# The second query projection of a decoder layer as a seven-product unit, placed behind the first scores

## The chip, the cores and the metric

One core of a Trainium2 chip runs the whole kernel. The metric is the device time of one execution in microseconds; the kernel before takes 1145.6 us (median of 3 runs, 1145.52 to 1145.76). Line numbers are those of the kernel before.

## The reference

One decoder layer on 512 tokens of width 1024 in float32: half a SwiGLU step, a token mixer, half a second SwiGLU step, and a gated per-layer embedding. The change is in the mixer:

```
h = rmsnorm(x, mix_norm);  z = h @ w_in
zq, zk, zv, zc, zg = split(z)            # 1024, 128, 128, 2048, 2048 columns
q = rope(rmsnorm(zq per head)); k = rope(rmsnorm(zk per head))
a = sliding_window_attention(q, k, zv, sinks) @ attn_proj     # 16 heads of 64, window 128
u = ca * sigmoid(cb); c = silu(layernorm(depthwise_conv(u, 31 taps))) @ conv_proj
x = x + (sigmoid(ga) * a + sigmoid(gb) * c) @ w_out
```

The 16 query heads are computed as two groups of 8 heads (g = 0 and 1), each a product of 512 tokens x 1024 features with 1024 x 512 weights.

## The kernel before

**Arithmetic.** A float32 product is made of three passes (`mm3`, line 758): every operand is split into a rounded high part and a remainder (`split_into`, line 718: one ScalarE copy, one VectorE subtraction), and high x high, high x low and low x high are added up in PSUM. Weights come in pieces of 128 x 1024 (512 KB): `piece` (line 733) loads one and splits it; for the keys named in `FLEX` (line 55), the queries among them, the subtraction goes to VectorE or GpSimd, whichever is free.

**Two ways to make a product.** `token_major` (line 1326) makes one directly: for each of 8 blocks k of 128 features and each of 4 token tiles, the activations are the weights of TensorE and 512 columns of the piece stream past. `unit` (line 987) makes a product of 2 x 2 blocks with seven block products in place of eight (in the manner of Strassen and Winograd). It loads four pieces, adds two of them together by accumulating DMAs on GpSimd's queue, makes two further sums on VectorE into PSUM tiles `zs`, and splits the seven weight forms. Its activations come as seven `forms`, which are sums of quarters of the input. Two accumulators a and b for each of two m, four PSUM banks, are filled step by step, and after each step the caller reads what is done (`yield`). With `turned=True` the token tile is TensorE's weight and 256 columns of the weight form stream past.

**The queries.** `queries(g)` (line 1418) uses `query_unit` (line 1377) for g = 0 and `token_major` with four pieces of `wq` for g = 1 (PSUM tile `q1b`, read by four ScalarE copies into `zq`). `query_unit` builds the forms of the mixer's input itself: the sums `mix_t4` to `mix_t7` of quarters of the scaled input, split into `mix_f`, and the parts of `h2` (the trace calls them `mix_h`). It then runs the unit named `wq0` (PSUM tiles `wq_a`, `wq_b`, `zs_wq`) and scales its results by the norm's factor into `zq`. In both ways `heads_rsqrt` (line 1301: four squares on ScalarE, four sums on VectorE and some fifteen tiny steps) and `rope` (line 1316: GpSimd) follow. `scores` (line 1436) transposes a token tile of `zq` and multiplies it with the keys; it takes one bank and then four. `softmax` (line 1483) and `values` (line 1503) follow. The convolution (`conv`, line 1279) of five blocks of 128 channels is a chain of 31 VectorE steps each in a PSUM bank (`cz`, at most two at once), and that of three (`POOLCH`) is made of ScalarE products and GpSimd sums. `conv_norm` (line 1578) adds the blocks (`ln_acc`), takes the mean (`ln_mb`) and the variance (`ln_v`), and makes the operand `cv` of the projection `cp`.

**Order.** The code first records all operations of the program as a list. `ORDER` (line 40) says in which order the mixer's steps are recorded: K keys and values, a and b the two conv projections of a block, Q queries, A scores, E softmax, V values, g and h the two gates, p attention projection, L the layer norm. A planner (`plan`, line 676) then simulates the list with a cost for each operation and due times taken back from the matmuls (`deadlines`, line 378); TensorE's next group is the first of the next 10 (`WINDOW`) whose operands and banks are there, and the other engines take the most urgent ready operation. Buffers are numbered slots (`SLOTS`, line 686): 70 activation tiles of 128 x 512, four raw pieces, four high and four low weight pieces, two raw pieces of kind k, 8 PSUM banks. The planner repeats this in a few passes, keeps the best, and the real program is issued in the order of its start times. So a changed step changes the place of any other.

**Layout.** `_layout` (line 1783) stores the weights in the host's memory in the order in which pieces are read. For the first query group (`wq[:4]`) these are the four blocks of the 2 x 2 product; for the second they are rows of 512 columns.

Of the kernel before, what the change touches and what calls it, by code (L numbers as in the profile page):

```python
# [16 lines left out]
P = 128  # L17
S = 512
NT = S // P
D = 1024  # L20
# [3 lines left out]
NH = 16  # L24
NKV = 2
HD = 64
# [7 lines left out]
PIECE = 1024  # L34
# [3 lines left out]


ORDER = """  # L40
K0 a0 b0 a1 b1 Q0 A0 a3 a2 A1 b2 E0 E1 b3 A2 E2 a4 V0 A3 a5 E3 V1 b4 Q1 V2 b5
V3 A5 a7 A6 g5 h7 A4 E5 A7 E6 E4 V6 g3 a6 E7 g0 V5 b6 V4 g4 g6 V7 h1 g2 h4 b7
g1 p0 p2 g7 p3 L0 p4 h3 p7 h2 p5 p1 p6 h5 h0 h6
"""
# [365 lines left out]
CUT = 4  # L410
PLAIN = 6, 4
MID = 20, 20
DOWNS = {8: [(0, 4)], 20: [(4, 11)]}
SPARE = 0, 1, 2, 4

# [273 lines left out]
def record():  # L689
# [74 lines left out]
    def part(w, s):  # L764
        return w[0][:, s], w[1][:, s]
# [608 lines left out]

    zq, rq = {}, {}

    def query_unit(g):

        forms = {f: [] for f in range(1, 8)}
        for q in range(2):  # L1380
            t5, t6, t7, t4 = (ftile(f"mix_t{n}_{q}") for n in (5, 6, 7, 4))
            for j in range(2):
                k, v = 2 * q + j, slice(j * HS, (j + 1) * HS)
                xg = ftile(f"mix_xg{k}")
                nc.scalar.activation(xg, x[k], AF.Copy, scale=g_mix[:, k : k + 1])
                gb, xb = g_mix[:, k + 4 : k + 5], x[k + 4]
                nc.flex.tensor_tensor(t5[:, v], xg[:, lo_], xg[:, hi_], op=ALU.subtract)
                nc.vector.scalar_tensor_tensor(t6[:, v], xb[:, hi_], gb, t5[:, v], op0=ALU.mult, op1=ALU.add)
                nc.vector.scalar_tensor_tensor(t7[:, v], xb[:, hi_], gb, xg[:, hi_], op0=ALU.mult, op1=ALU.subtract)
                nc.vector.scalar_tensor_tensor(t4[:, v], xb[:, lo_], gb, t6[:, v], op0=ALU.mult, op1=ALU.subtract)  # L1390
                for f, i, t in ((1, k, lo_), (2, k + 4, lo_), (3, k + 4, hi_)):
                    forms[f].append(part(h2[i], t))
            for f, t, sign in ((5, t5, None), (6, t6, -1.0), (7, t7, None), (4, t4, -1.0)):
                parts = split(f"mix_f{f}_{q}", t, sign)
                for j in range(2):
                    forms[f].append(part(parts, slice(j * HS, (j + 1) * HS)))

        def src(b):
            return Dram("wq")[4 * g + 2 * (b // 10 - 1) + b % 10 - 1]

        for t in range(NT):
            zq[g, t] = ftile(f"zq{g}_{t}")
        for f, m, b1, b2 in unit(f"wq{g}", src, PIECE, lambda k, m: k * HS, forms, turned=True):
            z0, z1 = zq[g, m], zq[g, m + 2]
            r0, r1 = (r2k[:, t : t + 1] for t in (m, m + 2))
            if f == 1:
                nc.scalar.activation(z0[:, lo_], b1, AF.Copy, scale=r0)
                nc.vector.scalar_tensor_tensor(z0[:, lo_], b2, r0, z0[:, lo_], op0=ALU.mult, op1=ALU.add)
            elif f == 6:
                nc.scalar.activation(z1[:, lo_], b2, AF.Copy, scale=r1)  # L1410
                nc.scalar.activation(z1[:, hi_], b1, AF.Copy, scale=minus[:, m + 2 : m + 3])
            elif f == 7:
                nc.vector.scalar_tensor_tensor(z1[:, lo_], b1, r1, z1[:, lo_], op0=ALU.mult, op1=ALU.add)
                nc.vector.scalar_tensor_tensor(z1[:, hi_], b2, minus[:, m + 2 : m + 3], z1[:, hi_], op0=ALU.mult, op1=ALU.add)
            else:
                nc.scalar.activation(z0[:, hi_], b2, AF.Copy, scale=minus[:, m : m + 1])

    def queries(g):

        if g == 0:  # L1420
            query_unit(g)
        else:
            pss = token_major(f"q{g}", "wq", 4 * g, 4, 2, S)
            for t in range(NT):
                z = zq[g, t] = ftile(f"zq{g}_{t}")
                nc.scalar.activation(z, pss[t], AF.Copy, scale=r2k[:, t : t + 1])
        z3s = [zq[g, t].rearrange("p (h d) -> p h d", d=HD) for t in range(NT)]
        rq[g] = heads_rsqrt(f"q{g}", z3s, 8, HD**-0.5, False)
        for t in range(NT):
            rope(f"q{g}_{t}", z3s[t], 8, qcs, t)  # L1430
# [237 lines left out]
    forms = {f: [] for f in range(1, 8)}  # L1668
# [25 lines left out]
    for oo in range(1):  # L1694
# [6 lines left out]
        for f, m, b1, b2 in steps:  # L1701
            o = 2 * oo + m
# [80 lines left out]
def _layout(inputs):  # L1783

    import numpy as np

    f = {k: np.asarray(v) for k, v in inputs.items()}

    def feat(v):
        return v.reshape(KD, P).T  # L1790

    def kxn(w):

        kt, nt = w.shape[0] // P, w.shape[1] // P
        return w.reshape(kt, P, nt, P).transpose(2, 1, 0, 3).reshape(nt, P, kt * P)

    def wgu(w):
        v = w.reshape(2, 4, P, 2, KF, P)
        return v.transpose(4, 0, 2, 1, 3, 5).reshape(2 * KF, P, PIECE)

    def wdown(w):


        v = w.reshape(KF // 2, 2, P, 2, 2, 2, P)
        out = np.zeros((24, P, 8, P), np.float32)
        out[:8] = v[:4].transpose(4, 3, 1, 2, 5, 0, 6).reshape(8, P, 8, P)
        out[8:, :, :7] = v[4:].transpose(4, 5, 3, 1, 2, 0, 6).reshape(16, P, 7, P)
        return out.reshape(24, P, PIECE)

    order = [h for j in range(NPAIR) for h in (j, j + NPAIR)]  # L1810
    win = f["w_in"][0]
    o = np.cumsum([0, NH * HD, NKV * HD, NKV * HD, 2 * D, 2 * D])
    wq = win[:, : o[1]].reshape(D, NH, HD)[:, order].reshape(4, 2, P, 2, S)
    wq = wq.transpose(3, 0, 2, 1, 4).reshape(8, P, PIECE)
    w0 = win[:, : o[1]].reshape(D, NH, HD)[:, order][:, :8].reshape(2, 4, P, 2, S // 2)
    wq[:4] = w0.transpose(3, 0, 2, 1, 4).reshape(4, P, PIECE)
    wkv = win[:, o[1] : o[3]].reshape(2, 4, P, 2 * P).transpose(0, 2, 1, 3).reshape(2, P, PIECE)

    def pairs(w):
        t = kxn(w)  # L1820
        n = t.shape[0] // 2
        return t.reshape(2, n, *t.shape[1:]).transpose(1, 0, 2, 3).reshape(t.shape)

    wap = f["attn_proj"][0].reshape(NH, HD, D)[order].reshape(NH * HD, D)

    half = HD // 8
    inv = np.float32(500000.0) ** (-np.arange(0, 16, 2, dtype=np.float32) / np.float32(16))
    ang = np.arange(S, dtype=np.float32)[:, None] * inv[None, :].astype(np.float32)
    cos, sin = np.cos(ang), np.sin(ang)
    cs = np.stack([np.concatenate([cos, cos], 1), np.concatenate([-sin, sin], 1)], 1)  # L1830
    cs = cs.astype(np.float32).reshape(NT, P, 2, 2 * half).transpose(1, 0, 2, 3)

    qi, kj = np.arange(W)[:, None], np.arange(W)[None, :]
    masks = np.where(kj > qi, -1e30, 0.0).astype(np.float32)

    rows = lambda v: np.broadcast_to(v, (P, v.shape[-1]))
    gains = np.stack(
        [
            feat(f[k][0])
            for k in (  # L1840
                "ffn1_norm", "mix_norm", "ffn2_norm", "ple_gate_norm",
                "ple_norm", "dw_b", "conv_ln_g", "conv_ln_b",
            )
        ],
        1,
    )
    arrays = {
        "xT": f["x"][0].T.reshape(KD, P, S),
        "pT": f["p"][0, 0].T.reshape(KP, P, S),
        "gains": gains,  # L1850
        "wgu1": wgu(f["ffn1_wgu"][0]),
        "wd1": wdown(f["ffn1_wdown"][0]),
        "wgu2": wgu(f["ffn2_wgu"][0]),
        "wd2": wdown(f["ffn2_wdown"][0]),
        "wq": wq,
        "wkv": wkv,
        "wzc": pairs(win[:, o[3] : o[4]]),
        "wzg": pairs(win[:, o[4] : o[5]]),
        "gq": rows(f["q_norm"][0]),
        "gk": rows(f["k_norm"][0]),  # L1860
        "sinks": rows(f["sinks"][0][order]),
        "wap": kxn(wap),
        "dww": f["dw_w"][0].T.reshape(KD, P, TAPS).transpose(1, 0, 2),
        "wcp": kxn(f["conv_proj"][0]),
        "wout": f["w_out"][0].reshape(2, 4, P, 2, 2, 2, P).transpose(4, 3, 0, 2, 5, 1, 6).reshape(8, P, PIECE),
        "wple": kxn(f["ple_proj"][0]).reshape(2, 4, P, KP * P).transpose(0, 2, 1, 3).reshape(2, P, PIECE),
        "wgate": np.concatenate(
            [
                f["ple_gate_w"][0].reshape(2, 4, P, 2, 2, 2, P).transpose(4, 3, 0, 2, 5, 1, 6).reshape(8, P, PIECE)[:4],
                kxn(f["ple_gate_w"][0])[[2, 3, 6, 7]],  # L1870
            ]
        ),
        "cs": cs,
        "masks": masks,
    }
    return {k: np.ascontiguousarray(v) for k, v in arrays.items()}
# [19 lines left out]
```

## Time and profile before

| | us |
|---|---|
| median of 3 runs | 1145.6 |
| the profiled execution | 1145.5 |
| its span | 1143.8 |
| TensorE (PE) busy | 1135.7 |
| VectorE (DVE) busy | 1000.4 |
| ScalarE (ACT) busy | 743.0 |
| GpSimd (POOL) busy | 457.8 |

The span is the time from the first to the last instruction in the trace; some 1.7 us lie around it. All instructions bear one line (1778), where the planned list is issued, so groups are told apart by tiles. In the trace the first feed-forward step ends near 345 us, the mixer near 705, its output product follows, and the second feed-forward step ends near 1083. A matmul's printed duration includes its pipeline, so successive matmuls overlap and the spacing of starts is what counts.

### The profile page before, as it was taken

To read this page: it belongs to the slowest core of one execution; us is meant where nothing else is said; L and a number is where in the kernel's file an instruction comes from. 1 tells how busy PE (TensorE), PEld (TensorE's weight loads), DVE (VectorE), ACT (ScalarE), POOL (GpSimd) and SP (SyncE) were. 2 spreads that over 40 slices of the span, in tenths; PEclk is the share of its full clock that TensorE was granted. 3 is DMA by queue.
4 is the path that set the end of the run, shared out by engine and by line. 5 is a ranking of instruction groups with operands and counts; after the bars stand their busy time and mean duration, and the time that the engine had idled before them with its cause. 6 is when DMAs were issued, how large, how long until landed. Compare 5 with 4: busy or idle time off the path is not lost.

```text
span 1143.8 us, 20799 instructions
## 1 busy us (share of the span) xinstructions
PE 1135.7 (99%) x7804; PEld 1054.2 (92%) x7804; DVE 1000.4 (87%) x1701; ACT 743.0 (65%) x1332; POOL 457.8 (40%) x531
## 2 busy tenths in 40 slices
PE   9999999999999999999999999999999999999998
PEld 8899999999999988888888888988999999999997
DVE  7799978889887799997997779989998788899897
ACT  7656456665557889999975654655663566565682
POOL 1632113322112896976688124035231132131156
PEclk9999999999999999999999999999999999999999
DMA  7456666665658481664644554436666666656643
GB/s 242 126 162 148 165 160 163 151 144 151 157 132 208 119 206 38 173 158 97 162 129 131 146 148 108 114 108 169 145 164 151 150 167 148 168 119 178 152 117 99
DMA packets 54821, 167.92 MB, mean 147 GB/s; under 512 B 6592, under 2 KB 14400, under 8 KB 54720
## 3 DMA queue, kind: packets, MB, share of 16 engines
q1 hardware_dynamic: 39888, 114.12, 30.2%
q0 software_dynamic: 14688, 52.44, 26.6%
q8 instruction: 61, 1.00, 0.4%
q14 instruction: 40, 0.33, 0.1%
q10 hardware_dynamic: 144, 0.03, 0.0%
HBM read 145.59 MB, written 2.10 MB: 129 GB/s over the span
## 4 chain that ended last, share of the span: by engine, by line
PE 97%; DVE 3%; issue 0%; ACT 0%; ACTq 0%
PE wgu_b L1778 17%; PE wgu_a L1778 13%; PE wd_b L1778 10%; PE wd_a L1778 8%; PE f_g L1778 5%; PE f_u L1778 5%; PE gb L1778 4%; PE ga L1778 4%; PE ap L1778 4%; PE cp L1778 4%; PE ca L1778 3%; PE cb L1778 3%; PE wout_b L1778 2%; PE pg L1778 2%; PE q1b L1778 2%; PE wout_a L1778 2%
## 5 line engine op out<-in xcount | busy, mean ns | idle before, releaser
L1778 DVE TENSOR_TENSOR wlo_wgu<-raw_wgu,whi_wgu 128x1024 fp32r<-128x1024 f32 (+1 forms) x141 | 140.4, 1010 | 27.1 <-ACT whi_wgu L1778 26.8
L1778 ACT ACTIVATE whi_wgu<-raw_wgu 128x1024 fp32r<-128x1024 f32 (+1 forms) x141 | 115.4, 838 | 69.8 <-PE wgu_b L1778 34.7
L1778 POOL TENSOR_TENSOR y<-y,ct 128x511 f32<-128x511 f32 (+26 forms) x90 | 112.0, 1319 | 14.1 <-ACT ct L1778 5.3
L1778 PE MATMUL wgu_b<-f_t_h,wlo_wgu 128*128 128x256 f32 x408 | 115.5, 283 | 0.0
L1778 PE MATMUL wgu_b<-f_t_h,whi_wgu 128*128 128x256 f32 x408 | 115.5, 283 | 0.0
L1778 PE MATMUL wgu_b<-f_t_l,whi_wgu 128*128 128x256 f32 x408 | 115.5, 283 | 0.0
L1778 ACT ACTIVATE whi_wd<-raw_wd 128x896 fp32r<-128x896 f32 (+1 forms) x60 | 59.3, 989 | 73.3 <-PE wd_b L1778 41.5
L1778 DVE SCALAR_TENSOR_TENSOR cz<-u,dww,cz 128x504 f32<-128x504 f32 (+28 forms) x145 | 104.7, 733 | 2.0
L1778 POOL DMA_DIRECT2D raw_wgu<-in_wgu x34 | 29.7, 878 | 153.3 <-DMA raw_wgu<-in_wgu 78.6
L1778 PEld LDWEIGHTS wgu_b<-f_t_h,wlo_wgu 128*128 128x128 f32 x408 | 78.3, 192 | 0.0
L1778 PEld LDWEIGHTS wgu_b<-f_t_h,whi_wgu 128*128 128x128 f32 x408 | 78.3, 192 | 0.0
L1778 PEld LDWEIGHTS wgu_b<-f_t_l,whi_wgu 128*128 128x128 f32 x408 | 78.3, 192 | 0.0
L1778 DVE TENSOR_TENSOR wlo_wd<-raw_wd,whi_wd 128x896 fp32r<-128x896 f32 (+1 forms) x60 | 70.8, 1180 | 7.2 <-ACT whi_wd L1778 6.8
L1778 PE MATMUL wgu_a<-f_nh,wlo_wgu 128*128 128x256 f32 x272 | 77.0, 283 | 0.0
L1778 PE MATMUL wgu_a<-f_nh,whi_wgu 128*128 128x256 f32 x272 | 77.0, 283 | 0.0
L1778 PE MATMUL wgu_a<-f_nl,whi_wgu 128*128 128x256 f32 x272 | 77.0, 283 | 0.0
L1778 PE MATMUL wd_b<-f_f_h,wlo_wd 128*128 128x256 f32 x264 | 75.1, 285 | 1.2 <-DVE x L1778 1.2
L1778 PE MATMUL wd_a<-f_f_h,wlo_wd 128*128 128x256 f32 x264 | 74.7, 283 | 0.0
L1778 PE MATMUL wd_a<-f_f_h,whi_wd 128*128 128x256 f32 x264 | 74.7, 283 | 0.0
L1778 PE MATMUL wd_b<-f_f_l,whi_wd 128*128 128x256 f32 x264 | 74.7, 283 | 0.0
L1778 PE MATMUL wd_b<-f_f_h,whi_wd 128*128 128x256 f32 x264 | 74.7, 283 | 0.0
L1778 PE MATMUL wd_a<-f_f_l,whi_wd 128*128 128x256 f32 x264 | 74.7, 283 | 0.0
(625 smaller groups left out, 4278.6 us busy)
## 6 DMA issues: line engine op xcount, KB each, us to landing
raw_wgu<-in_wgu SPq DMA_DIRECT2D x76, 512.0 KB, 4.5
raw_wgu<-in_wgu POOLq DMA_DIRECT2D x34, 512.0 KB, 5.5
raw_wd<-in_wd SPq DMA_DIRECT2D x32, 448.0 KB, 4.0
raw_wd<-in_wd SPq DMA_DIRECT2D x16, 512.0 KB, 4.4
raw_wzc<-in_wzc SPq DMA_DIRECT2D x16, 512.0 KB, 3.9
wlo_wzc<-raw_wzc POOLq DMA_DIRECT2D x16, 512.0 KB, 4.9
raw_wzg<-in_wzg SPq DMA_DIRECT2D x16, 512.0 KB, 3.5
wlo_wzg<-raw_wzg POOLq DMA_DIRECT2D x16, 512.0 KB, 4.5
```

The lines of the kernel that those rows point to most:

```text
L1778: made[op] = getattr(engines[op.eng], op.what)(*a, **k)
```

## The change

`ORDER` has Q1 directly behind A0, the first group of scores, in place of a position 16 steps later behind b4. The forms of the mixer's input move into a function `mix_forms` that makes them once, at the first call, and hands the same tiles to each later one. `queries` takes the unit for both groups (`QUNITS`). `_layout` stores the weights of both groups as four blocks of the 2 x 2 product. The planner, its costs and its slots are as before.

```diff
--- before.py
+++ after.py
@@ -38,7 +38,7 @@
 
 
 ORDER = """
-K0 a0 b0 a1 b1 Q0 A0 a3 a2 A1 b2 E0 E1 b3 A2 E2 a4 V0 A3 a5 E3 V1 b4 Q1 V2 b5
+K0 a0 b0 a1 b1 Q0 A0 Q1 a3 a2 A1 b2 E0 E1 b3 A2 E2 a4 V0 A3 a5 E3 V1 b4 V2 b5
 V3 A5 a7 A6 g5 h7 A4 E5 A7 E6 E4 V6 g3 a6 E7 g0 V5 b6 V4 g4 g6 V7 h1 g2 h4 b7
 g1 p0 p2 g7 p3 L0 p4 h3 p7 h2 p5 p1 p6 h5 h0 h6
 """
@@ -410,6 +410,7 @@
 CUT = 4
 PLAIN = 6, 4
 MID = 20, 20
+QUNITS = 0, 1
 DOWNS = {8: [(0, 4)], 20: [(4, 11)]}
 SPARE = 0, 1, 2, 4
 
@@ -1374,9 +1375,14 @@
 
     zq, rq = {}, {}
 
-    def query_unit(g):
-
-        forms = {f: [] for f in range(1, 8)}
+    mixf = {}
+
+    def mix_forms():
+
+        if mixf:
+            return mixf
+        mixf.update({f: [] for f in range(1, 8)})
+        forms = mixf
         for q in range(2):
             t5, t6, t7, t4 = (ftile(f"mix_t{n}_{q}") for n in (5, 6, 7, 4))
             for j in range(2):
@@ -1394,6 +1400,11 @@
                 parts = split(f"mix_f{f}_{q}", t, sign)
                 for j in range(2):
                     forms[f].append(part(parts, slice(j * HS, (j + 1) * HS)))
+        return forms
+
+    def query_unit(g):
+
+        forms = mix_forms()
 
         def src(b):
             return Dram("wq")[4 * g + 2 * (b // 10 - 1) + b % 10 - 1]
@@ -1417,7 +1428,7 @@
 
     def queries(g):
 
-        if g == 0:
+        if g in QUNITS:
             query_unit(g)
         else:
             pss = token_major(f"q{g}", "wq", 4 * g, 4, 2, S)
@@ -1812,8 +1823,9 @@
     o = np.cumsum([0, NH * HD, NKV * HD, NKV * HD, 2 * D, 2 * D])
     wq = win[:, : o[1]].reshape(D, NH, HD)[:, order].reshape(4, 2, P, 2, S)
     wq = wq.transpose(3, 0, 2, 1, 4).reshape(8, P, PIECE)
-    w0 = win[:, : o[1]].reshape(D, NH, HD)[:, order][:, :8].reshape(2, 4, P, 2, S // 2)
-    wq[:4] = w0.transpose(3, 0, 2, 1, 4).reshape(4, P, PIECE)
+    for g in QUNITS:
+        w0 = win[:, : o[1]].reshape(D, NH, HD)[:, order][:, 8 * g : 8 * g + 8].reshape(2, 4, P, 2, S // 2)
+        wq[4 * g : 4 * g + 4] = w0.transpose(3, 0, 2, 1, 4).reshape(4, P, PIECE)
     wkv = win[:, o[1] : o[3]].reshape(2, 4, P, 2 * P).transpose(0, 2, 1, 3).reshape(2, P, PIECE)
 
     def pairs(w):
```

## The prediction

> **What bounds the kernel now.** I read the page first: engine shares, clock, chain.
>
> ```profile
> span 1143.8 us, 20799 instructions
> PE 1135.7 (99%) x7804; PEld 1054.2 (92%) x7804; DVE 1000.4 (87%) x1701; ACT 743.0 (65%) x1332; POOL 457.8 (40%) x531
> PEclk9999999999999999999999999999999999999999
> PE 97%; DVE 3%; issue 0%; ACT 0%; ACTq 0%
> ```
>
> TensorE is busy for all but 8.1 us of 1143.8 with the granted clock at 9 tenths or more in every slice, and the chain that ended last is 97% PE. So the time is the sum of the matmuls, and an edit pays only by what it takes from that sum or from its few holes. The second view is the busy time in stretches of the mixer, where the change lies (columns: stretch, length, busy us of PE, PEld, DVE, ACT, POOL with instruction counts, granted clock, DMA share, GB/s).
>
> ```profile
> core 0: us, PE busy (x) PEld busy (x) DVE busy (x) ACT busy (x) POOL busy (x), PEclk, DMA share, GB/s
> 386.00:430.00 44.00, 42.97 (x288) 37.88 (x287) 43.51 (x81) 38.36 (x59) 41.04 (x49) 1.00 0.74 180
> 430.00:483.00 53.00, 52.88 (x281) 43.62 (x280) 50.80 (x91) 52.76 (x137) 40.42 (x61) 1.00 0.42 108
> 483.00:536.00 53.00, 53.00 (x320) 43.94 (x319) 49.26 (x109) 52.40 (x130) 39.47 (x71) 1.00 0.54 125
> 536.00:546.00 10.00, 10.00 (x50) 8.35 (x49) 4.66 (x11) 9.92 (x25) 4.79 (x9) 1.00 0.63 144
> 546.00:582.00 36.00, 36.00 (x165) 29.82 (x164) 33.57 (x54) 33.40 (x60) 27.68 (x25) 1.00 0.54 142
> 582.00:619.00 37.00, 37.00 (x165) 30.66 (x164) 36.26 (x50) 22.87 (x32) 33.07 (x29) 1.00 0.53 147
> ```
>
> PE has holes of 1.03 and 0.12 us here and none later. But VectorE is close to full itself: it has 0.49 us free of 44 in the first row, and 14.9 us free in the 233 us of all six (233 less 218.07). ScalarE has 6.6 us free from 386 to 546 (160 less 153.44) and 14.1 in the last row. The waits of PE name the hole of the first row:
>
> ```profile
> PE ca L1778 <- DVE s L1778: 0.9, 1, 0.9
> ```
>
> A conv projection could not start until VectorE had emptied the banks of first scores.
>
> **What the change takes from PE.** In the chain (start, us, what) the plain second projection and pieces of the turned first one can be compared:
>
> ```profile
> 460.67 21.79 PE q1b L1778 x96
> 388.18 2.88 PE wq_a L1778 x24
> 398.26 5.47 PE ca L1778 x24
> ```
>
> The old one is 8 inputs k x 3 passes x 4 token tiles = 96 matmuls of 512 columns, 21.79 us, 227 ns each. A turned unit is 7 products x 2 token tiles x 4 k x 3 passes = 168 matmuls of 256 columns; at 2.88/24 = 120 ns each that is 20.16 us. The term is 21.79 - 20.16 = 1.63 us less. The gain is small because two matmuls of 256 columns cost 240 ns against 227: seven eighths of the columns, but 12/13 of the time. A seam between a unit and another group costs little (a conv block behind the unit took 5.47, which at 24 x 227 ns would be 5.45), so I add nothing for it.
>
> [...]
>
> **What it adds elsewhere.** Rows by tile (min/median/max ns, first and last start):
>
> ```profile
> L1778 DVE TENSOR_TENSOR wlo_wq<-raw_wq,whi_wq x8: 1215/1474/2310, 366.5 to 471.6; 128x1024 fp32r<-128x1024 f32 x8
> L1778 POOL TENSOR_TENSOR wlo_wq<-raw_wq,whi_wq x1: 2405/2405/2405, 458.4 to 458.4; 128x1024 fp32r<-128x1024 f32 x1
> L1778 DVE TENSOR_TENSOR wlo_wq<-zs_wq,whi_wq x4: 681/684/691, 369.9 to 391.9; 128x512 fp32r<-128x512 f32 x4
> L1778 DVE TENSOR_TENSOR zs_wq<-raw_wq,raw_wq x2: 695/695/695, 362.7 to 363.7; 128x512 f32<-128x512 f32 x2
> L1778 DVE TENSOR_TENSOR zs_wq<-raw_wq,zs_wq x2: 686/688/690, 371.8 to 375.4; 128x512 f32<-128x512 f32 x2
> L1778 DVE SCALAR_TENSOR_TENSOR zq<-wq_b,mix_n_r,zq x2: 472/474/475, 385.6 to 389.4; 128x256 f32<-128x256 f32 x2
> L1778 ACT ACTIVATE whi_wq<-raw_wq x9: 1045/1052/1170, 365.3 to 462.7; 128x1024 fp32r<-128x1024 f32 x9
> L1778 ACT ACTIVATE whi_wq<-zs_wq x4: 586/596/615, 369.3 to 387.7; 128x512 fp32r<-128x512 f32 x4
> L1778 ACT ACTIVATE zq<-wq_a,mix_n_r x2: 452/457/462, 384.3 to 386.8; 128x256 f32<-128x256 f32 x2
> L1778 ACT ACTIVATE zq<-q1b,mix_n_r x4: 677/682/688, 481.0 to 482.7; 128x512 f32<-128x512 f32 x4
> L1778 POOL DMA_DIRECT2D raw_wq<-in_wq x2: 882/885/888, 350.3 to 368.1; - x2
>   POOL raw_wq L1778: 2.1, 1
> ```
>
> VectorE: a unit splits five stored pieces (5 x 1.215 to 1.474) and two summed ones in halves (4 x 0.684), makes the sums (2 x 0.695 + 2 x 0.688) and folds six results (6 x 0.474): 14.4 to 15.7 us. The plain projection split four pieces; nine rows above less the first unit's five leave three on VectorE and one on POOL, so 3 x 1.215 to 3 x 2.310 = 3.6 to 6.9 us go. VectorE gets 7.5 to 12.1 us more; I take 9.5, between the two. ScalarE: 5 x 1.052 + 4 x 0.596 + 8 x 0.457 = 11.3 against 4 x 1.052 + 4 x 0.682 = 6.9, so 4.4 more. POOL loses the 2.405 split and gets two issues of accumulating DMAs, 2 x 0.885: 0.6 less, but each sits in POOL's queue until the raw piece has landed, which cost 2.1 us once and holds the convolution adds behind it; POOL is at 41.04 of 44 in the first stretch. These have no reader on PE that soon, so I set them at nothing, cover being the conv's later work. DMA: 6 transfers of 0.5 MB for 4, pulled ahead of the next conv weights in SP's queue; the share there is 0.74, and the unit displaces conv blocks that draw DMA too. Nothing, again.
>
> The sums of the mixer's input are made once either way and cost nothing more; they stay allocated for one more unit.
>
> **What moves.** With the unit go the squares, reductions and rotary work of its four token tiles, some 50 us ahead:
>
> ```profile
> L1778 ACT ACTIVATE q_sq<-zq x8: 614/631/637, 397.7 to 489.0; 128x512 f32<-128x512 f32 x8
> L1778 DVE TENSOR_REDUCE q_v<-q_sq x8: 673/678/689, 398.9 to 490.5; 128x8 f32<-128x512 f32 x8
> L1778 POOL TENSOR_TENSOR q_w<-zq,qcs x16: 457/562/1585, 396.5 to 490.5; 128x64 f32<-128x64 f32 x16
> ```
>
> Half of each: 2.5 us of ScalarE, 2.7 of VectorE, 4.5 of POOL and more small ones. VectorE, already at 43.51 of 44, thus gets some 17 us of new work around 410 to 440. Convolution taps and the softmax of the first heads are queued behind it, and run later. PE does not notice as long as it has other groups: the unit itself is 20 us of matmuls, and conv and gate blocks of 5.4 us wait in the list. What is lost early is a debt of 9.5 us on VectorE, to be paid out of its 14.9 us free. It comes due where the convolution ends, at the layer norm:
>
> ```profile
> 618.05 0.75 DVE L1778 SCALAR_TENSOR_TENSOR y<-u,dww,cz 128x511 f32<-128x511 f32 x1
> 625.00 0.69 DVE L1778 TENSOR_TENSOR ln_s_l<-ln_acc,ln_s_h 128x512 fp32r<-128x512 f32 x1 [3.74 <-ACT ln_s_h L1778]
> ```
>
> ```profile
> 614.78 10.88 PE gb L1778 x48
> 625.66 5.45 PE ap L1778 x24
> 631.10 0.46 PE ln_mb L1778 x2
> 631.56 10.92 PE ap L1778 x48
> 644.16 5.61 PE gb L1778 x24
> 650.22 10.88 PE gb L1778 x48
> 661.10 2.95 PE cp L1778 x13
> ```
>
> The mean's operand is ready at 625.69 and PE takes it at 631.10: 5.4 us to spare. From there to the projection that needs the normed result at 661.10 are 30 us, covered by five blocks (10.92 + 5.61 + 10.88). Debt less free time less slack: 9.5 - 14.9 - 5.4 is negative, so the likeliest price is nothing, and what is late next is nobody.
>
> **Sum.** Against the profiled execution, 1145.5 us of which 1143.8 are the span: 1145.5 - 1.63 = 1143.9. The median is 0.1 above that execution: 1145.6 - 1.63 = 1144.0. A change of 0.2% (2.3 us) is about what a measurement of this kernel can tell from none, so 1143.3 to 1147.9 count as no change, and the forecast lies inside. The 0.9 us hole is left as it is: the scores that cause it still come in that stretch.
>
> **Rivals.**
>
> The holes go too. The first scores' wait of 0.9 us belongs to one order of groups; with a 20 us unit to fill in just there it may vanish. 1.63 + 0.9 = 2.5: 1143.1. For: PE then has a ready group at that place. Against: the unit occupies four PSUM banks, and the wait was for banks. Bounds: with the last tenth of the second row gone too, 1142.9.
>
> The layer norm becomes late (slower). The free time of VectorE is partly time in which it waits for ScalarE, as the 3.74 us before the mean's operand. If only 4 of the 14.9 us can be used, the convolution ends 5.5 us late or more. It decides from 5.4 us on: then one block of 5.44 us slides in front of the mean and is missing behind it, and the last projection waits up to 5.4 us. 1144.0 + 5.4 = 1149.4; a part of it gives 1147 or 1148. For: ScalarE, which paces the softmax, has only 6.6 us free to 546 and gets 4.4. Against: a free stretch of 5.3 us on VectorE at 536 to 546 lies ahead of the last two convolutions.
>
> Waits inside the unit. Its products accumulate in banks that ScalarE and VectorE must read between steps; each is nearly full, and one two-microsecond split ahead of a read stops PE for some tenths. A few such waits, as long as the 0.9 us already seen, give the gain back: two make 1145.8, four 1147.6.
>
> Weight loads pace the shorter matmuls.
>
> ```profile
> L1778 PEld LDWEIGHTS wq_b<-wlo_wq,mix_f_h x24: 188/192/192, 386.7 to 406.2; 128*128 128x128 f32 x24
> ```
>
> If each matmul took as long as its load, 168 x 0.192 = 32.3 us, 10.5 more than now: 1156.1. The row of 24 in 2.88 us speaks against it, since loads there overlap. [...]
>
> The plan is redone as a whole and the new order gets another place than the diff says, or other groups move: a hole of a microsecond anywhere, either sign, 1143 to 1147.
>
> **Chances.** Forecast 0.48 (own range 1143.3 to 1145.3; 0.46 no change, 0.02 faster). Holes go 0.20 (0.18 faster, 0.02 none). Layer norm 0.18 (0.16 slower, 0.02 none). Waits in the unit 0.10 (0.07 none, 0.03 slower). Weight loads 0.01 slower. Other plan 0.03 (0.01 none, 0.02 slower). Sum: faster 0.20, same 0.58, slower 0.22. The range takes the bounds of the two larger rivals, 1142.9 to 1149.4.
>
> **What would show it.** Right: 168 matmuls of 256 columns on the unit's tiles in some 20.2 us and no 512-column ones; PE busy 1.6 us less; VectorE's share up by 7.5 to 12 us in the mixer; the mean's matmuls within 5 us of 631 and the following projection without a wait. Wrong: waits of PE over 1 us in the mixer, on the projection behind the layer norm (second rival), on the unit's banks (third), or matmuls of 256 columns spaced over 125 ns (fourth). It would also be wrong if PE's holes in the feed-forward stages change, which this argument holds fixed.

## The result, and the profile after

The changed kernel takes 1155.9 us (median of 4 runs, 1155.22 to 1156.36) against 1145.7 for the kernel before in the same job (4 runs): a ratio of 1.0089, with a 95% interval of 1.0071 to 1.0106. The forecast was 1144.0, the range 1142.9 to 1149.4. The time lies 6.5 us above its upper end.

The page of the profile after, an execution of 1155.7 us (span, busy time by engine, clock in 40 slices, the chain by engine):

```profile
span 1153.9 us, 20968 instructions
PE 1142.2 (99%) x7876; PEld 1057.6 (92%) x7876; DVE 1016.5 (88%) x1723; ACT 751.5 (65%) x1345; POOL 448.8 (39%) x526
PEclk9999999999999999999999999999999999999999
PE 84%; ACT 8%; DVE 6%; issue 1%; DMA 0%; POOL 0%; SPq 0%; ACTq 0%; DVEq 0%; POOLq 0%
```

The span is 10.1 us longer. PE still reads 99%, but the chain that ended last now runs 8% on ScalarE and 6% on VectorE, where it was 97% PE. So PE waits for others in places that the first two lines don't show. The tenths of the clock show nothing either: a drop of 3.41 us, as it turns out below, is lost in a slice of 29.

The mixer in the stretches of the prediction (same columns; the row of 536 to 582 answers to two rows of before):

```profile
core 0: us, PE busy (x) PEld busy (x) DVE busy (x) ACT busy (x) POOL busy (x), PEclk, DMA share, GB/s
386.00:430.00 44.00, 43.80 (x352) 42.14 (x351) 42.59 (x76) 38.44 (x64) 39.51 (x54) 1.00 0.57 149
430.00:483.00 53.00, 50.96 (x279) 41.19 (x278) 49.15 (x98) 51.47 (x118) 41.93 (x61) 0.97 0.61 142
483.00:536.00 53.00, 51.00 (x304) 41.46 (x303) 50.97 (x104) 51.22 (x135) 28.80 (x50) 1.00 0.58 133
536.00:582.00 46.00, 46.00 (x214) 38.13 (x213) 43.22 (x75) 45.62 (x92) 32.06 (x42) 1.00 0.55 138
```

In the first row the unit runs nearly without a stop (PE lacks 0.20 us of the 44), and the 0.9 us hole of before is gone. In the second and third PE has 2.0 us of holes each, and in the second the granted clock is 0.97. GpSimd is busy for 28.80 us of the third row, where it was 39.47. It does less there, so something holds it up.

**The first loss: softmax.** PE's waits between 455 and 500 us (engine, tile, releaser: total, times, longest):

```profile
PE pT L1789 <- ACT s L1789: 1.3, 2, 1.1
PE pT L1789 <- DVE s L1789: 1.0, 1, 1.0
PE pT L1789 <- POOL sg L1789: 0.8, 1, 0.8
...
```

These, and the few tenths left out, all stand before `pT`, the transposes of the probabilities. PE's timeline across the longest, and the stretch behind it by windows:

```profile
474.18 0.33 PE L1789 MATMUL pT<-ident,s 128*128 128x128 f32 x1 [1.14 <-ACT s L1789]
475.30 0.63 PE L1789 MATMUL pT<-ident,s 128*128 128x128 f32 x4 [0.79 <-POOL sg L1789]
475.97 0.58 PE L1789 MATMUL cb<-mix_h_h,wlo_wzc 128*128 128x512 f32 x1
476.35 0.63 PE L1789 MATMUL cb<-mix_h_h,whi_wzc 128*128 128x512 f32 x1
...
480.19 0.39 PE L1789 MATMUL cb<-mix_h_l,whi_wzc 128*128 128x512 f32 x1
```

```profile
476.24:479.65 3.41, 3.41 (x9) 2.64 (x9) 3.41 (x7) 3.41 (x9) 3.41 (x7) 0.50 0.14 58
```

Sixteen transposes that need 16 x 0.109 us (109 ns from start to start in the kernel before) take from 470.90 to 475.97, which is 3.3 us too long. Right behind them TensorE gets half its clock (0.50) for 3.41 us: the matmuls of the conv gate last 0.63 us instead of 0.39 and stand 0.43 apart instead of 0.227. The block of 24 takes 7.17 us from start to start in place of 5.45, another 1.7. A second hole of the same kind, ahead of and between eight transposes from 495 to 499, costs 2.4 by the same count, and one at 521 costs 0.4.

**The second loss: the layer norm.** The rows that answer to those of the prediction: VectorE's last convolution step, GpSimd's last sum; then the chain; then PE's weight loads for the projection behind the norm.

```profile
622.46 0.74 DVE L1789 SCALAR_TENSOR_TENSOR y<-u,dww,cz 128x511 f32<-128x511 f32 x1
```

```profile
638.17 1.29 POOL L1789 TENSOR_TENSOR ln_acc<-ln_acc,ln_acc 128x512 f32<-128x512 f32 x1
```

```profile
642.45 0.46 PE ln_mb L1789 x2
642.91 5.48 PE ap L1789 x24
648.39 5.44 PE gb L1789 x24
...
655.50 5.62 PE gb L1789 x24
...
673.46 0.53 ACT cv_h L1789
...
674.83 39.27 PE cp L1789 x172
```

```profile
PEld cp L1789 <- DVE cv_l L1789: 3.0, 7, 0.5
PEld cp L1789 <- ACT cv_h L1789: 1.9, 6, 0.3
```

VectorE ends its part of the convolution 4.4 us later than before, GpSimd 15.2 us later: the same sum in the kernel before is this row.

```profile
623.01 1.29 POOL L1778 TENSOR_TENSOR ln_acc<-ln_acc,ln_acc 128x512 f32<-128x512 f32 x1
```

The mean moves from 631.10 to 642.45, past blocks of the gates and of the attention projection that lay behind it. Four blocks of 5.4 us are left behind it (the fourth, from 661.40, is not in the chain), where five were, and the projection overtakes the operand that it reads: `cp` first starts at 666.84 and takes 47.1 us, where it took 43.5. That is 3.6 us.

**The ledger.** To the start of `cp` (660.94 before, 666.84 after) the loss is 5.9. Holes and half clock make 3.3 + 1.7 + 2.4 + 0.4 = 7.8; with some 0.35 us inside the unit (by the spacing of starts) and 0.3 that the mixer begins later, 8.5. Off go the unit's 1.63 and the old hole's 0.93, and 5.9 is left. With 3.6 in `cp` and 0.6 behind the mixer it is the 10.1 of the span.

### The profile page after: what moved, and what is told of

Its sections match the earlier page's. It is cut to its first block, busy times and chain, and to the rows that moved or that the text cites. A ratio compares the mean times of both kernels' runs of the same rounds, so it can differ in the third digit from the quotient of the medians.

```text
span 1153.9 us, 20968 instructions
## 1 busy us (share of the span) xinstructions
PE 1142.2 (99%) x7876; PEld 1057.6 (92%) x7876; DVE 1016.5 (88%) x1723; ACT 751.5 (65%) x1345; POOL 448.8 (39%) x526
## 4 chain that ended last, share of the span: by engine, by line
PE 84%; ACT 8%; DVE 6%; issue 1%; DMA 0%; POOL 0%; SPq 0%; ACTq 0%; DVEq 0%; POOLq 0%
PE wgu_b L1789 16%; PE wgu_a L1789 12%; PE wd_b L1789 10%; PE wd_a L1789 8%; PE f_g L1789 4%; PE f_u L1789 4%; PE ap L1789 4%; PE cp L1789 3%; PE gb L1789 3%; PE ga L1789 3%; PE cb L1789 3%; ACT s L1789 2%; PE wout_b L1789 2%; PE pg L1789 2%; PE wout_a L1789 1%; PE wq_a L1789 1%
## 5 line engine op out<-in xcount | busy, mean ns | idle before, releaser
L1789 POOL TENSOR_TENSOR y<-y,ct 128x507 f32<-128x507 f32 (+28 forms) x90 | 113.7, 1307 | 11.8 <-ACT ct L1789 2.9
L1789 DVE SCALAR_TENSOR_TENSOR cz<-u,dww,cz 128x504 f32<-128x504 f32 (+25 forms) x145 | 104.6, 732 | 1.7
```

The lines of the kernel that those rows point to most:

```text
L1789: made[op] = getattr(engines[op.eng], op.what)(*a, **k)
```

## The experiments

After the result I set two theories against each other. *Load*: the unit's added work on VectorE and ScalarE, now early, is what softmax waits for. *Place*: the 20 us of matmuls that the old place gave PE as cover are missing there. The first four runs fitted neither well, so a third came up. *Order*: `ORDER` fits the kernel before; any edit makes the planner lay out another list, with new holes of PE, and a halved clock as that at 476.24 (1.7 us) makes some of them dearer.

**The two parts alone.** First the move with the plain projection, then the unit at the old place:

```diff
-QUNITS = 0, 1
+QUNITS = 0,
```

> The order of the change with the second query projection made directly, as before (four pieces, 96 matmuls of 512 columns): the move alone. Theory of the place (the 20 us of matmuls no longer stand at 460 to 482 us as cover while ScalarE is full of softmax, and the conv gates behind the second queries start some 20 us later, so that GpSimd's convolutions end later): 1153 to 1158 us, holes of PE between 455 and 500, and a wait at the projection behind the layer norm. Theory of the load (the 9.5 us of VectorE and 4.4 of ScalarE that the unit adds are what is paid): 1145 to 1148.

```diff
-K0 a0 b0 a1 b1 Q0 A0 Q1 a3 a2 ... V1 b4 V2 b5
+K0 a0 b0 a1 b1 Q0 A0 a3 a2 ... V1 b4 Q1 V2 b5
```

> The second query projection as a unit at its old place behind the fifth conv gate: the unit alone. Theory of the place: the cover stays where it was, 1144 to 1146.5 us. Theory of the load: the unit's extra work falls into the stretch where ScalarE and VectorE have least to spare, 1149 to 1156.

The move alone took 1159.05 us (ratio 1.0113, 1.0092 to 1.0134), the unit alone 1155.7 (1.0085, 1.0068 to 1.0102). Each alone loses as much as both together or more, so the loss is no sum of a price of the unit and a price of the place. The unit alone lies in the range of *load*: 3.6 us of PE's waits there stand before the unit's own matmuls, most of them for VectorE. The move alone lies above both ranges. It has the wait at the projection that *place* asked for, but between 455 and 500 us PE waits for 0.3 us in all. The waits of PE in the mixer are different ones in each. The two longest of the unit at the old place:

```profile
PE pT L1789 <- DVE of L1789: 2.2, 2, 1.6
PE o L1789 <- DVE p_l L1789: 1.6, 1, 1.6
```

and of the move alone, with its windows, whose clock is some 5 us of its loss (the execution at the highest mean clock, 0.999, took 1156.26):

```profile
PE sc L1789 <- DVE qT_l L1789: 1.4, 1, 1.4
PE qTp L1789 <- POOL zq L1789: 1.3, 1, 1.3
...
404.20:417.80 13.60, 12.64 (x68) 10.91 (x69) 11.47 (x28) 8.74 (x15) 10.98 (x12) 0.50 0.44 117
```

Both holes lie between 400 and 418 us (PE lacks 1.64 us from 400.0 to 404.1 and 0.96 in the row above), and TensorE gets half its clock for 13.6 us. In this profile `cp` waits as it does in after (47.1 us), and with the unit at the old place it doesn't (43.5).

**ScalarE relieved.** The list of after as it stands, with ScalarE products of the convolution ahead of the holes left out:

```diff
+LEFT = {f"ct0_{d}" for d in range(13, 28)}
...
+            if op.eng == "ACT" and name in LEFT:
+                continue
```

> The changed kernel in its own order of instructions, less 15 ScalarE products of the first GpSimd convolution (taps 13 to 27 of block 0, some 10 us of ScalarE between 408 and 449 us); GpSimd adds the input itself in their place, so those taps lack their weights. If PE's holes between 470 and 500 us are softmax late on ScalarE: they shrink by at least two thirds with the low clock behind them, 1148 to 1151 us, and the 3.5 us at the projection behind the layer norm stay. If they come from banks, weights or GpSimd: 1154 or more.

1156.03 us (1.0088, 1.0068 to 1.0108): nothing gained, though its profile has a second drop of the clock that the profile of after has not (0.96 over 485 to 500 us, where after reads 1.00). From 386 to 430 ScalarE had 3.3 us less to do (the row below against 38.44), from 430 to 470 4.6 us less (35.25 against 39.87), and the hole stood where it stood:

```profile
386.00:430.00 44.00, 43.80 (x352) 42.14 (x351) 42.57 (x76) 35.16 (x59) 39.48 (x54) 1.00 0.58 149
```

```profile
474.17 0.33 PE L1798 MATMUL pT<-ident,s 128*128 128x128 f32 x1 [1.18 <-ACT s L1798]
```

What ScalarE had less to do from 405 to 470 it spent waiting, longest for VectorE (3.1 us, before a square of the queries) and for PE (3.0, before a weight copy into a buffer that PE still read). So it is not a backlog of ScalarE's convolution work from the time ahead that makes the hole. The order of each engine's instructions is that of after. ScalarE, for one, makes a weight copy, loads a table and makes a sigmoid ahead of the two rows of probabilities for which PE waits (timeline of ScalarE in after):

```profile
470.82 1.07 ACT L1789 ACTIVATE whi_wzc<-raw_wzc 128x1024 fp32r<-128x1024 f32 x1
471.91 1.28 ACT L1789 ACT_TABLE_LOAD   x1
473.21 0.63 ACT L1789 ACTIVATE sg<-sg 128x512 f32<-128x512 f32 x1
473.74 0.68 ACT L1789 ACTIVATE s<-s,den 128x128 f32<-128x128 f32 x2
```

So load falls for ScalarE. VectorE, which gets more of the unit's work, was not relieved: it is busy for 38.92 of the 40 us from 430 to 470.

**ScalarE loaded.** The other way round: the list of before as it stands, with seven products of the convolution made twice, and then with three.

```diff
+TWICE = {f"ct0_{d}" for d in range(10, 17)}
...
+            if op.eng == "ACT" and name in TWICE:
+                made[op] = getattr(engines[op.eng], op.what)(*a, **k)
```

> The kernel before in its own order, with 7 of those ScalarE products (block 0, taps 10 to 16, about 4.9 us of ScalarE between 400 and 420 us) made twice: the load that the unit adds on ScalarE, without the unit. If ScalarE has no slack there that PE would not feel: 1148 to 1150 us. If the order's cover takes it up: 1145 to 1147.

```diff
-TWICE = {f"ct0_{d}" for d in range(10, 17)}
+TWICE = {f"ct0_{d}" for d in range(14, 17)}
```

> The kernel before in its own order with 3 ScalarE products made twice (block 0, taps 14 to 16, some 2.1 us of ScalarE before 420 us) in place of 7. With 7 PE had a hole of 2.5 us and then ran at half clock for 6.8 us. If the clock falls only behind a hole of some length: a hole of about 1 us, no half clock, 1145.5 to 1147. If ScalarE has no slack at all and any hole drops the clock: 1148 to 1150.

Seven products of 0.70 us cost 4.4 us (1150.19; 1.0040, 1.0024 to 1.0056), three cost 0.7, which the interval does not tell from nothing (1146.31; 1.0005, 0.9995 to 1.0015). The first conv gate behind the first scores, with seven and the windows behind it, and then with three:

```profile
422.72 0.80 PE L1782 MATMUL cb<-mix_h_h,wlo_wzc 128*128 128x512 f32 x1 [2.46 <-DVE s L1782]
...
422.11:428.94 6.83, 6.22 (x15) 4.93 (x16) 6.29 (x16) 3.71 (x6) 6.11 (x7) 0.50 0.63 156
```

```profile
420.73 0.50 PE L1782 MATMUL cb<-mix_h_h,wlo_wzc 128*128 128x512 f32 x1 [0.78 <-DVE s L1782]
```

Within this fixed list a delay of ScalarE (7 x 0.70 us) did reach PE, as a hole of 2.46 us where before has none over 0.9. And that hole costs more than itself: behind it the block of 24 takes 8.58 us in place of 5.45, which is 3.1 more. Behind 0.78 us the matmuls keep their 0.39.

**One step moved, no work changed.** The kernel before, with Q1 one step later:

```diff
-K0 a0 b0 a1 b1 Q0 A0 a3 a2 A1 b2 E0 E1 b3 A2 E2 a4 V0 A3 a5 E3 V1 b4 Q1 V2 b5
+K0 a0 b0 a1 b1 Q0 A0 a3 a2 A1 b2 E0 E1 b3 A2 E2 a4 V0 A3 a5 E3 V1 b4 V2 Q1 b5
```

> The work of the kernel before, nothing added, with the second queries one step later in the order (behind the third values instead of in front of them). Theory of the fitted order (the order of the kernel before was chosen for its own plan, and any edit that makes the planner plan anew loses some microseconds to new holes of PE): 1147 to 1153 us. Theories of the place or of the load: one step moves neither, 1145 to 1146.5.

1151.52 us (1.0051, 1.0036 to 1.0066): 5.9 us for nothing but a place in a list. PE's waits are again others; the two largest:

```profile
PE pT L1789 <- DVE s L1789: 2.7, 2, 1.6
PE cb L1789 <- DVE of L1789: 1.4, 1, 1.4
...
```

**Other steps fitted to the unit.** If the loss comes from the list, another list should give it back at the same load and place. I let the planner price many orders with the unit directly behind A0, and took the best that it found; then the same order with the plain projection.

```diff
-K0 a0 b0 a1 b1 Q0 A0 Q1 a3 a2 A1 b2 E0 E1 b3 A2 E2 a4 V0 A3 a5 E3 V1 b4 V2 b5
...
+K0 a0 b0 a1 b1 Q0 A0 Q1 a3 a2 A1 b2 E1 b3 A2 E2 a4 E0 V0 A3 a5 E3 V1 b4 A5
+b5 V3 a7 V2 A6 h7 g5 A4 A7 E5 E6 E4 E7 V6 g3 a6 g2 g0 V5 b6 V4 g4 g6 V7 b7
+h1 h4 p0 g1 g7 p3 h3 p2 p4 p7 L0 p1 h2 p5 p6 h5 h0 h6
```

> The changed kernel (both projections as units, the second right behind the first scores) with the other steps of the mixer's order fitted anew for it: step order alone, no work added or taken away. Theory of the fitted order: the unit's gain comes out less what holes are left, 1143 to 1147 us. Theories of the place or of the load: place and load are those of the change, so 1152 to 1157.

> That same newly fitted order with the second projection made directly. Theory of the fitted order: an order fitted to the unit does not fit the direct product, 1152 to 1162 us. If the new order were simply a better one: 1144 to 1147.

With the unit 1147.95 us (11 runs, 1146.69 to 1149.42; 1.0019, 1.0010 to 1.0028): 8 of the 10 us are back, with all of the unit's work and the unit at its place. It is 1 us above the range that *order* gave, and 2.3 slower than before. With the plain projection in the same order 1157.17 (1.0100, 1.0081 to 1.0118). In this list the plain projection is 9 us slower than the unit, in that of before 10 us faster. What is left with the unit is one hole, and the half clock behind it:

```profile
473.79 1.09 PE L1789 MATMUL pT<-ident,s 128*128 128x128 f32 x4 [1.95 <-DVE s L1789]
...
473.73:477.14 3.41, 3.35 (x12) 3.09 (x13) 3.38 (x7) 3.41 (x8) 2.32 (x4) 0.50 0.19 47
```

**The test of it.** If order is all, the work of before should run as fast in another fitted list, and the change should do its harm to that one as well. The first kernel is the kernel before with a new order, the second repeats the change under study on it, the third is the unit in yet another order.

```diff
-K0 a0 b0 a1 b1 Q0 A0 a3 a2 A1 b2 E0 E1 b3 A2 E2 a4 V0 A3 a5 E3 V1 b4 Q1 V2 b5
...
+K0 a0 b0 a1 b1 Q0 A0 a3 a2 A1 b2 A2 E0 E2 E1 b3 a4 V0 A3 a5 E3 V1 Q1 b4 V2
+b5 A5 h7 V3 a7 A6 g5 A7 A4 E5 E6 E4 V6 g3 a6 E7 g0 h3 V5 b6 V4 g4 g6 g1 V7
+h1 g2 b7 h4 p0 p2 p3 g7 L0 p7 h2 p5 h0 p4 p6 h6 h5 p1
```

> The work of before, plain projection included, with other steps of the order moved (Q1 stands one step ahead of b4 instead of behind it, A2, E2, A5, h7, h3, g1 and the last steps elsewhere). Theory 'order' (every list has holes of its own; the one of before is merely a good list, and another good list is as good): 1143 to 1146, with no hole of PE over 1.5 us in the mixer and no row of half clock; the projection behind the layer norm starts without a wait. Theory 'place' (the list of before is the only one that suits these engines, any moved step costs some microseconds): 1149 or more, as the move by one step was.

```diff
-K0 a0 b0 a1 b1 Q0 A0 a3 a2 A1 b2 A2 E0 E2 E1 b3 a4 V0 A3 a5 E3 V1 Q1 b4 V2
+K0 a0 b0 a1 b1 Q0 A0 Q1 a3 a2 A1 b2 A2 E0 E2 E1 b3 a4 V0 A3 a5 E3 V1 b4 V2
...
-QUNITS = 0,
+QUNITS = 0, 1
```

> The change under study repeated on the other order of the run beside it: Q1 goes directly behind A0 as a turned unit, all other steps as there. Theory 'order': what made the loss was that one step was moved in a list that fitted without it, so the loss comes back here, 5 to 11 us over the run beside it, but not by the same holes as in after: waits of PE on scores and transposes at other places, and again blocks short behind the mean. Theory 'before's list was a fluke' (the loss belongs to before's list alone): within 2 us of the run beside it.

> The unit directly behind A0, with the other steps moved once more (against the first refitted order: V2, A6, h7, g5 around the fourth group of conv blocks and p0, p1, p2, h3, g7 at the end). Theory 'order and clock': 1145 to 1148.5; the rest of the loss is one hole of some 2 us at 470 to 476 and, in those executions where the clock is halved behind it, 1 to 2 us more; the granted clock of the executions runs with their times, about 1.1 us for each 0.001. Against before the unit's 1.6 us are eaten by that hole. If the hole is gone on the chip: 1143.5 to 1144.5. Theory 'load' (the added VectorE and ScalarE work stands on the path wherever the steps are): 1150 or more.

The three took 1145.30 us (0.9997, 0.9988 to 1.0005), 1153.68 (1.0068, 1.0054 to 1.0081) and 1147.87 (1.0019, 1.0010 to 1.0028). So there are two lists for the old work that differ in many steps and whose times the interval does not tell apart, and the change costs 8.4 us on the new one, 10.2 on the old. Its holes there are not those of after. The only wait of PE over 0.4 us in the mixer of the first, then the two longest of the second, and the block ahead of its mean:

```profile
PE qTp L1789 <- DVE y L1789: 0.5, 1, 0.5
```

```profile
PE wq_b L1789 <- DVE zq L1789: 2.0, 1, 2.0
PE ga L1789 <- DVE p_l L1789: 1.1, 1, 1.1
...
628.26 4.54 DMA wlo_wzg<-raw_wzg
...
632.84 5.74 PE gb L1789 x24
638.58 0.46 PE ln_mb L1789 x2
```

My expectation for the second had blocks missing behind the mean again. That did not come: `cp` takes 43.5 us there, and a gate block waited for its weights ahead of the mean instead. The third kernel has the hole of the first refitted one in another guise (1.8 us before the transposes of the queries, at 475), and waits of 0.9, 0.9 and 0.5 us beside it. No list that I found with the unit directly behind A0 is free of it.

## Why the prediction was wrong

**What held.** The unit is 168 matmuls of 256 columns at 120 ns, as forecast (24 of them in 2.88 us), and runs nearly without a stop; the 1.63 us are real. The old hole did go, as the first rival said. In the changed kernel the rivals of waits inside the unit (0.35 us) and of weight loads (24 matmuls still take 2.88 us) are out. VectorE took on about what was worked out: the rows of the whole mixer, before and after, show 10.5 us more for it (9.5 forecast). ScalarE has 8.1 more (4.4 forecast) and GpSimd 4.1 less (0.6 forecast). ScalarE's sum had no term for table loads: there are 13 of 1.28 us in place of 9, one of them ahead of the probabilities at 474. Their number follows the list and not the work (13 in the move by one step, 9 in the refitted unit), but the time does not follow it (9 in the unit at the old place, 11 in the refitted old work).

```profile
345.70:704.50 358.80, 357.66 (x1893) 301.66 (x1892) 310.33 (x562) 285.80 (x564) 235.71 (x304) 1.00 0.55 140
346.00:713.90 367.90, 363.58 (x1964) 304.92 (x1963) 320.86 (x577) 293.89 (x577) 231.59 (x301) 1.00 0.55 138
```

(The first row is of the kernel before.)

**The step that failed: "PE does not notice as long as it has other groups".** The prediction listed what is queued behind the unit and priced it at nothing, since conv and gate blocks wait in the list. PE did have them, but it takes its groups in the planned order, and that order was taken to stay as it is. It doesn't: with both units one behind the other from 381 to 424, broken only by the first scores, the scores of the next three tiles start at 441, 454 and 469 in place of 426, 434 and 456. The softmax behind them is squeezed into the time in which ScalarE is full (39.87 us of the 40 from 430 to 470), and the old projection, which gave PE 21.8 us of cover from 460.67 to 482.46, is no longer there. The prediction named the work that would hide the unit at its new place, and not the work that the projection had hidden at its old one. What the step put at nothing is 6.1 us of holes (3.3 + 2.4 + 0.4). That the missing cover makes them is argued and not shown: the move alone lacks it too, and PE waits for 0.3 us there between 455 and 500. What the runs show is that the list makes them: the refitted unit has the same work at the same place, and one hole.

**The term that was not there: the clock.** From 5.9 to 1142.4 us the kernel before reads a granted clock of 1.00, and from 20 to 1083 its longest hole is 0.9 us. So a wait was priced at its own length. In after the drop (0.50 for 3.41 us) costs 1.7 us, and in the list of before with seven products doubled 3.1.

**"Debt less free time less slack negative ... what is late next is nobody".** The second rival has the mechanism: blocks slide ahead of the mean and are missing behind it, for 3.6 of its 5.4 us. But it put the debt on VectorE, which came 4.4 us late. The late one was GpSimd, whose account the prediction set "at nothing" as work with no reader on PE that soon. It could be read in the kernel before: the 3.74 us that VectorE waits for ScalarE ahead of the mean end in a wait of ScalarE for GpSimd's last sum.

```profile
624.33 0.63 ACT L1778 ACTIVATE ln_s_h<-ln_acc 128x512 fp32r<-128x512 f32 x1 [1.50 <-POOL ln_acc L1778]
```

So the convolution ended on GpSimd already, and VectorE's free time was not the account to ask. In the changed kernel GpSimd's work was less and its waits more, as its row between 400 and 600 us shows, before and after:

```profile
POOL den L1778 <- ACT es L1778: 12.9, 7, 4.6
```

```profile
POOL den L1789 <- ACT es L1789: 26.6, 7, 6.4
```

The sum of a softmax's denominator stands in GpSimd's queue until ScalarE has made its last exponential, and the convolution's additions stand behind it. The 13.7 us more of that are near the 12.1 by which GpSimd is less busy in those 200 us (145.57 for 157.68) and the 15.2 by which the convolution ends late. No run takes this wait away alone, and with the unit at the old place 20.9 us of it came with ScalarE products of the convolution that were only 3.0 us late (the last starts at 615.7 us, against 612.7 before and 628.8 in after); so it is argued and not shown that it is the whole cause.

**"The plan is redone as a whole ... a hole of a microsecond anywhere", chance 0.03.** This was the case that came, at ten times the price. The runs show why both numbers were too small: one step moved and no work changed costs 5.9 us; five kernels whose list was not fitted to their own work (the change, each part alone, the plain projection in the unit's list, the unit in the plain one's) lost 8 to 13 us. The kernel before has 8.1 us without work on PE in 1143.8, and in its mixer 1.1; a list with fewer holes can hardly be had, one with more can.

**What stays open.** Whether some list makes the unit pay its 1.6 us. The two best that I found end at 1147.9, with a longest hole of 1.8 to 1.95 us each. Nor is it known what part of that remainder is load: no run takes the unit's added work off VectorE. It also wasn't tried whether a changed order on ScalarE alone (the probabilities ahead of the table load) closes the hole of after.

## What to carry to other kernels

When a program is issued from a planned list, an edit buys a new list and not its own difference: price the list, by asking what the old place had hidden and which first use comes late at the new one, and expect a loss where the old list left almost no holes. Compare an edit with the old code only after the rest of the order has been fitted to each of them. And read an engine's account by what it waits for at the head of its list, not by its busy time: GpSimd got less work (4.1 us less in the mixer) and became late (15.2 us).

## What was not expected of the hardware

A hole of TensorE can cost more than its length: in after the half clock behind it adds 1.7 us, with seven products doubled 3.1. Behind holes the granted clock goes to 0.50 for 3.41 us (after, from 476.24; the refitted unit, from 473.73), 6.83 (seven products doubled, from 422.11) or 13.6 (the move alone, from 404.20, two holes); with the unit at the old place it is 0.79 over the 8 us from 444. Single holes of 0.78 (three products doubled), 1.42 and 1.59 (the move by one step) and 1.79 us (the last refitted list) left it at 1.00 in the executions profiled; those of 1.95 (the refitted unit) and 2.02 (the change on the other list) halved it, the latter 1.4 us after its end; one of 2.46 (seven products doubled) halved it for twice as long. Smaller ones lowered it too: in after no hole is over 1.2 us, and in the change on the other list it is 0.87 from 500 to 513 us, where PE lacks 1.73 us and waits for no more than 1.1 at once.

So what PE lacks does not tell alone: these 1.73 us lowered the clock, and 1.79 of the 12 from 470 to 482 in the last refitted list left it. What else decides is not shown.

The granted clock differs from execution to execution of one program. The move alone took 1161.0 and 1161.1 us at a mean granted clock of 0.994, 1157.1 at 0.998 and 1156.3 at 0.999: about 1 us for each 0.001. The refitted unit took 1146.7 to 1148.0 in its four executions at 1.000 and 1148.2 to 1149.4 in its four at 0.998. That list, with its hole of 1.95 us, thus has not one time but several; the kernel before and the refitted old work, with no hole over 0.9 us in the mixer, spread by about 1 us. Why it differs, one trace of each kernel cannot show.
